# One more pair of tiles by seven products ahead of a scan, and fewer fillers inside it

## The chip, the cores and the metric

The kernel runs on one core of a Trainium2 chip. Its time is the device time of one execution in microseconds (us). The engines are TensorE (PE, with its weight loads listed as PEld), VectorE (DVE), ScalarE (ACT), GpSimd (POOL) and SyncE (SP, which here only issues transfers).

## What is computed

One layer of a bidirectional encoder over 1024 positions of width 1024, all in float32. The input is normalised and multiplied by one wide matrix; its 56 column tiles of 128 feed several mixers at once.

```python
h    = rmsnorm(x, attn_norm_w)
proj = h @ w_in                       # 1024 x 8192 columns
glu_in, q, v, z_f, z_b, og, g_a, g_b = split(proj)
a = dwconv31(glu(glu_in)); a = silu(layernorm(a)) @ pw_w
o = scan_forward(q, v, z_f) + scan_backward(q, v, z_b)   # 8 heads of 128, chunkwise
b = (rmsnorm_per_head(o) * silu(og)) @ o_w
x = x + (sigmoid(g_a) * a + sigmoid(g_b) * b) @ w_out
x = x + (silu(dwconv3(h2 @ w_gate)) * (h2 @ w_up)) @ w_down,  h2 = rmsnorm(x)
out = rmsnorm(x, final_norm_w)
```

The 8 tiles of glu_in are made first. The change concerns how the other 56 tiles (q, og, v, z_f, z_b, g_a, g_b, 8 each) are shared out.

## The kernel before

A product of a weight tile and the activations is three matrix multiplications of 128x512 (mm3, lines 148 to 150): each operand is split into a coarse part and a remainder, and high x high, high x low and low x high are added. The split itself (split, line 124) is a copy on ScalarE and a subtraction on VectorE.

Output tiles are made in two ways. A plain tile (std_job) takes 2 halves of the positions x 8 blocks x 3 = 48 multiplications. A pair (pair_job) makes two tiles together by a scheme of Strassen's kind: seven products of half the depth, 7 x 4 x 3 = 84 multiplications where two plain tiles need 96. It needs sums of weight blocks (add, lines 295 to 301: on VectorE with `first`, else by accumulating DMAs issued from GpSimd), seven split operands and combinations of the products (copy at line 428, evac at line 784).

The work is cut into pieces: a piece of these tiles is six multiplications, so that a pair has 14 pieces and a plain tile 8. TensorE's order is written out by hand: a Stream hands out pieces, and code that has other work for TensorE calls fill(n) between its steps. A fraction of a piece is kept as owed until the next call. The order on the other engines is made by a planner from costs and due times.

The stages around the change, in order:

- The convolution of 31 taps over 4 channel tiles runs on VectorE (conv_steps, taps at line 1023). The loop calls s_pairs.fill(CONV_FILL) after each of its 124 steps; the LayerNorm that follows has fills of its own (LN_FILL, 5, LN_LAST, twice), and then the stream of pairs is drained. NPAIRS pairs are made here; todo, the list of the 56 tiles, is taken in order.
- What is left of todo becomes plain tiles (rest_jobs), and after them 8 tiles of the convolution's pointwise product, 4 pieces each. They are the fillers of the scan (dense).
- The scan handles 8 heads x 2 halves = 16 items. For each item scan_levels has three steps and scan_states two; after each of these five, between(FILL) hands out FILL filler pieces, advances the preparation of the next item (scan_base) and the outputs of the head before (scan_outputs). Per item, TensorE forms block products at several levels: small ones (level, line 1179), then blocks of 32 and of 64 (blocks, line 1262), which read keys kG and queries qF that VectorE has just doubled (double_keys and double_queries, line 1128); then it transposes the keys (line 1302), ScalarE copies them (line 1304), and TensorE forms the states (line 1311). A head's outputs follow (line 1352). The value tile is transposed and copied once per item (line 1454).
- Before the loop, dense.fill takes 7 + 14 pieces; after it, TAIL takes 10 and the rest is drained.

```python
jobs = collections.deque(in_pair(n) for n in range(1, NPAIRS))
for _ in conv_steps():
    s_pairs.fill(CONV_FILL)
...
rest = todo[2 * NPAIRS :]
rest_jobs = [std_job(in_cols(c), ND, h_std, e) for c, e in rest[:-2]]
...
def between(fill):
    dense.fill(fill)
    if ahead is not None:
        ahead.step(BASE_STEPS)
    pending.fill(1)
```

Of the kernel before, what the change touches and what calls it, by code (L numbers as in the profile page):

```python
# [16 lines left out]
AX = mybir.AxisListType  # L17

P = 128
FILL = 1.77  # L20
TAIL = ((1, 2), (1, 1), (2, 4), (2, 3))
CONV_FILL = 1.67
NPAIRS = 19
LN_FILL = 6
LN_LAST = 12
GLU_FIRST = 4
# [21 lines left out]
def tile_hybrid_encoder(  # L48
# [201 lines left out]
    def std_job(src, nk, acts, evac, halves=(0, 1), step=2):  # L250


        def prep():
            raw = raw_w(src, nk)
            return split(w_page(nk), w_page(nk), raw, V)

        def run(w, halves=halves):
            for half in halves:
                acc = bank("mm")
                for k in range(nk):  # L260
                    mm3(acc, w, acts(k, half), k, k == 0, k == nk - 1)
                    if k % step == step - 1 or k == nk - 1:
                        yield
                evac(half, acc)

        return prep, run
# [299 lines left out]
    def in_cols(c0):  # L566
        return w_cols(w_in, 0, ND, c0)
# [246 lines left out]
    def in_pair(n):  # L814
        (c0, e0), (c1, e1) = todo[2 * n], todo[2 * n + 1]
        evs = (e0, e1)
        return pair_job(
            in_cols(c0),
            in_cols(c1),
            NK2,  # L820
            lambda i: ht[i],
            p1,
            p1,
            lambda e, *quadrant: evs[e](*quadrant),
            first=n == 0 or n >= 14,
            columns=2,
        )

# [121 lines left out]
    h_combos()  # L950
    s_glu.fill(GLU_LATE)
    pair0 = in_pair(0)
    w_pair0 = pair0[0]()
    s_glu.drain()
# [51 lines left out]


    jobs = collections.deque(in_pair(n) for n in range(1, NPAIRS))
    jobs.appendleft((lambda: w_pair0, pair0[1]))
    s_pairs = Stream(run_jobs(jobs, 4))  # L1010

    def conv_steps():
        for j in (3, 0, 1, 2):
            acc = p1.tile([P, S], F32, tag="ca", name=nm("acc"), bufs=2)
            g = gl[j]

            def tap(k):
                return vec("cdw", k * NCW + j)

            V.tensor_scalar(acc, g[:, 0:S], tap(0), vec("cb", j), op0=ALU.mult, op1=ALU.add)  # L1020
            yield
            for k in range(1, CK):
                V.scalar_tensor_tensor(  # L1023
                    acc, g[:, k : k + S], tap(k), acc, op0=ALU.mult, op1=ALU.add
                )
                yield
            for half in range(2):
                nc.sync.dma_start(d_cv[j][half], acc[:, half * H : (half + 1) * H])

    for _ in conv_steps():  # L1030
        s_pairs.fill(CONV_FILL)

# [39 lines left out]

    rest = todo[2 * NPAIRS :]
    rest_jobs = [std_job(in_cols(c), ND, h_std, e) for c, e in rest[:-2]]
# [220 lines left out]
    def scan_states(i, kG, v, Tt, Sf, Sb):  # L1295

        half = i % 2
        kTs = []
        for d in range(2):
            b = bank("mm" if d else "tr")  # L1300
            for c in range(4):
                T.transpose(b[:, c * P : (c + 1) * P], kG[:, d, c * P : (c + 1) * P], ident)
            kT = page(hp, "kT", 2)
            A.copy(kT, b)
            kTs.append(kT)
        yield
        for d in range(2):
            u = bank("mm" if d else "sc")
            for c in range(4):
                sl = slice(c * P, (c + 1) * P)  # L1310
                T.matmul(u[:, sl], kTs[d][:, sl], v[:, c, :], start=True, stop=True)
            u4 = c4(u)
            if d == 0:
                for c in range(4 if half == 0 else 3):
                    nx = Sf[half][:, c + 1, :] if c < 3 else Sf[1][:, 0, :]
                    if half == 0 and c == 0:
                        V.tensor_copy(nx, u4[:, 0, :])
                    else:
                        V.scalar_tensor_tensor(
                            nx,  # L1320
                            Sf[half][:, c, :],
                            Tt[:, half, 0, c : c + 1],
                            u4[:, c, :],
                            op0=ALU.mult,
                            op1=ALU.add,
                        )
            else:

                A.copy(Sb[half][:, 0:3, :], u4[:, 1:4, :])
                if half == 1:  # L1330
                    A.copy(Sb[0][:, 3, :], u4[:, 0, :])
        yield
# [96 lines left out]
    for h in range(NH):  # L1429
# [4 lines left out]
        for half in range(2):  # L1434
# [5 lines left out]
# [5 lines that stand above are left out]
# [3 lines left out]
            for n, _ in enumerate(scan_levels(base, S_t, Tt[:, half])):  # L1448
                if n == 1:
# [4 lines left out]
                    A.copy(v.rearrange("p c e -> p (c e)"), b)  # L1454
                between(FILL)
            qF, kG = base[:2]
            for _ in scan_states(i, kG, v, Tt, Sf, Sb):
                between(FILL)
            kept.append((S_t, v, qF))
# [481 lines left out]
    n = starts[-1] - per_seven - 12  # L1941
# [49 lines left out]
```

## Time and profile before

| What | us |
|---|---|
| median of 3 runs | 1755.64 (1755.04 to 1755.79) |
| the profiled execution | 1754.85 |
| its span, from the first to the last instruction | 1753.0 |
| TensorE busy | 1715.2 (98%) |
| VectorE busy | 1253.1 (71%) |
| ScalarE busy | 819.9 (47%) |
| mean granted TensorE clock | 0.996 of full speed |

A row of a table by stages gives the stretch in us from the span's start, its length, the busy time and number of instructions of PE, PEld, DVE, ACT and POOL, then the granted clock, the mean busy share of the 16 DMA engines and GB/s. In a group of instructions stand the line, the engine, the operation, output<-inputs, shapes and count, then busy time and the mean of one in ns, and after the bar the engine's idle time just before them with what ended it. A row of waits reads: who waited, for whom, us in total, times, the longest. The time of a multiplication in the list (some 390 ns) covers a pipeline; how far apart two of them start is the price of one.

### The profile page before, as it was taken

The page shows a single profiled execution, that of the slowest core. Times are in us where ns is not written, and L with a number is a line of the kernel's source. Part 1 is how long each engine was busy: PE and PEld are TensorE (multiplying, and loading weights), DVE is VectorE, ACT ScalarE, POOL GpSimd, SP SyncE. Part 2 cuts the span into 40 slices and gives each one's busy share as a digit, 9 for nine tenths or more (in the row PEclk, how much of TensorE's full clock was granted, in tenths as well). Part 3 has the DMA queues.
Part 4 walks back from the last instruction along what each step waited for, and adds up shares of the span by engine and source line. Part 5 has one row for each costly group of instructions (what it writes and reads, how often), then busy time and mean ns, then how long its engine had stood idle before and what let it go on. Part 6 is the DMA issues. An engine that isn't in the chain of part 4 may idle for free. (4 is left out here: it accounts for less than half of the span.)

```text
span 1753.0 us, 30378 instructions
## 1 busy us (share of the span) xinstructions
PE 1715.2 (98%) x11806; PEld 1409.3 (80%) x11806; DVE 1253.1 (71%) x1919; ACT 819.9 (47%) x1528; POOL 170.0 (10%) x184
## 2 busy tenths in 40 slices
PE   8999999999999999999999999999999999999997
PEld 6878888887888788788878887888878888878775
DVE  5599999746678888788556466676667777548864
ACT  7444433334466667776342245444334334443333
POOL 2201111100000000000000002111111111000110
PEclk9999999999999999999999999999999999999998
DMA  8768888855663343446579465586768776634742
GB/s 288 239 162 185 195 189 199 207 158 171 205 198 110 117 130 124 125 125 201 172 259 318 139 205 192 151 167 140 167 151 185 169 178 147 206 120 124 184 88 96
DMA packets 338470, 301.76 MB, mean 172 GB/s; under 512 B 24975, under 2 KB 252055, under 8 KB 338327
## 3 DMA queue, kind: packets, MB, share of 16 engines
q1 hardware_dynamic: 284310, 261.02, 47.5%
q0 software_dynamic: 44800, 37.76, 14.9%
q10 hardware_dynamic: 9216, 1.05, 0.4%
q8 instruction: 92, 1.51, 0.4%
q14 instruction: 52, 0.42, 0.1%
HBM read 197.27 MB, written 84.67 MB: 161 GB/s over the span
## 5 line engine op out<-in xcount | busy, mean ns | idle before, releaser
L148 PE MATMUL mm<-hx,wp 128*128 128x512 f32 x1068 | 428.2, 401 | 4.2 <-ACT tm L835 2.3
L150 PE MATMUL mm<-hx,wp 128*128 128x512 f32 x1068 | 418.0, 391 | 2.3 <-DVE wp L124 2.2
L149 PE MATMUL mm<-hx,wp 128*128 128x512 f32 x1068 | 417.1, 391 | 0.5 <-DVE hx L124 0.5
L124 ACT CAST wp<-wr 128x1024 fp32r<-128x1024 f32 (+2 forms) x147 | 147.3, 1003 | 261.8 <-PE mm L149 115.0
L148 PEld LDWEIGHTS mm<-hx,wp 128*128 128x128 f32 x1068 | 201.0, 188 | 48.3 <-ACT tm L835 2.8
L150 PEld LDWEIGHTS mm<-hx,wp 128*128 128x128 f32 x1068 | 200.8, 188 | 47.6 <-DVE wp L124 4.7
L149 PEld LDWEIGHTS mm<-hx,wp 128*128 128x128 f32 x1068 | 201.2, 188 | 40.5 <-DVE hx L124 1.2
L124 DVE TENSOR_TENSOR wp<-wr,wp 128x1024 fp32r<-128x1024 f32 (+2 forms) x145 | 169.6, 1170 | 75.0 <-ACT wp L124 68.4
L1023 DVE SCALAR_TENSOR_TENSOR acc<-gl,v_b,acc 128x1024 f32<-128x1024 f32 x120 | 149.2, 1282 | 0.4
L428 ACT COPY su<-mm 128x512 f32<-128x512 f32 x82 | 47.6, 581 | 65.2 <-PE mm L150 65.2
L1128 DVE TENSOR_TENSOR qF<-qF,tb 128x512 f32<-128x512 f32 x96 | 65.2, 687 | 11.7 <-ACT A L1160 11.7
L148 PE MATMUL tr<-hx,wp 128*128 128x512 f32 x180 | 70.5, 392 | 0.0
L124 ACT CAST wq<-sw 128x1024 fp32r<-128x1024 f32 x41 | 43.1, 1051 | 58.3 <-PE mm L149 43.0
L150 PE MATMUL tr<-hx,wp 128*128 128x512 f32 x180 | 70.1, 389 | 0.0
L149 PE MATMUL tr<-hx,wp 128*128 128x512 f32 x180 | 70.0, 389 | 0.0
L1618 DVE SCALAR_TENSOR_TENSOR tm<-gp,v_a,tm 128x512 f32<-128x512 f32 x88 | 66.0, 750 | 4.2 <-ACT tm L1616 2.0
L1128 DVE TENSOR_TENSOR kG<-kG,tb 128x512 f32<-128x512 f32 x96 | 65.7, 687 | 3.8 <-PE sc L1262 3.8
L148 PE MATMUL mm<-hy,wp 128*128 128x512 f32 x164 | 64.5, 393 | 0.0
L149 PE MATMUL mm<-hy,wp 128*128 128x512 f32 x164 | 64.2, 392 | 0.0
L148 PE MATMUL sc<-hy,wq 128*128 128x512 f32 x164 | 64.2, 392 | 0.0
L150 PE MATMUL sc<-hy,wq 128*128 128x512 f32 x164 | 64.2, 391 | 0.0
L149 PE MATMUL sc<-hy,wq 128*128 128x512 f32 x164 | 63.8, 389 | 0.0
(372 smaller groups left out, 3571.9 us busy)
## 6 DMA issues: line engine op xcount, KB each, us to landing
wr<-in_w_in_dram SPq DMA_DIRECT2D x48, 512.0 KB, 4.7
wr<-in_ffn_w_up_dram SPq DMA_DIRECT2D x22, 512.0 KB, 4.5
sw<-in_w_in_dram SPq DMA_DIRECT2D x38, 256.0 KB
d_g<-ft SPq DMA_DIRECT2D x38, 256.0 KB, 3.3
sw<-in_ffn_w_up_dram SPq DMA_DIRECT2D x38, 256.0 KB, 3.4
sw<-in_ffn_w_up_dram POOLq DMA_DIRECT2D x19, 512.0 KB, 8.4
wr<-sw POOLq DMA_DIRECT2D x32, 256.0 KB, 3.4
wr<-wr POOLq DMA_DIRECT2D x32, 256.0 KB, 3.9
```

The lines of the kernel that those rows point to most:

```text
L124: parts = A.copy(hi, src), eng.tensor_tensor(lo, src, hi.bitcast(F32), op=ALU.subtract)
L148: T.matmul(acc, whi[:, k, :], ahi, start=first, stop=False, skip_group_check=again)
L149: T.matmul(acc, whi[:, k, :], alo, start=False, stop=False, skip_group_check=again)
L150: T.matmul(acc, wlo[:, k, :], ahi, start=False, stop=last, skip_group_check=again)
L428: A.copy(t, acc)
L1023: V.scalar_tensor_tensor(acc, g[:, k : k + S], tap(k), acc, op0=ALU.mult, op1=ALU.add)
L1128: V.tensor_tensor(o, a, b, op=op)
L1618: V.scalar_tensor_tensor(c, g[:, o + k : o + k + H], vec("fdw", k * NF + j), c, op0=ALU.mult, op1=ALU.add,)
```

## The change

Twenty pairs are made ahead of the scan instead of 19; the tiles that move are z_f and z_b of the last head, which were the first two fillers. So 16 plain tiles instead of 18 stay as fillers, 160 pieces in all instead of 176, and each step of the scan hands out 1.56 pieces instead of 1.77. The convolution's steps hand out 1.78 pieces instead of 1.67. The pairs whose weight sums are made on VectorE are 0 and 15 to 19 instead of 0 and 14 to 18; pair 14's sums are now made by DMA.

```diff
-FILL = 1.77
+FILL = 1.56
 TAIL = ((1, 2), (1, 1), (2, 4), (2, 3))
-CONV_FILL = 1.67
-NPAIRS = 19
+CONV_FILL = 1.78
+NPAIRS = 20
...
             lambda e, *quadrant: evs[e](*quadrant),
-            first=n == 0 or n >= 14,
+            first=n == 0 or n >= 15,
             columns=2,
```

## The prediction

> **What bounds the kernel now.** First the head of the page, then busy time by stage.
>
> ```profile
> span 1753.0 us, 30378 instructions
> PE 1715.2 (98%) x11806; PEld 1409.3 (80%) x11806; DVE 1253.1 (71%) x1919; ACT 819.9 (47%) x1528; POOL 170.0 (10%) x184
> ```
>
> TensorE (PE) is the only engine that is busy nearly throughout. The change moves work from one stage into another, so I read the two stages separately: the stretch in which the pairs run beside the convolution and its LayerNorm (100 to 500 us), and the scan's loop over 16 items (519 to 856 us, from the first to the last copy of v at L1454).
>
> ```profile
> core 0: us, PE busy (x) PEld busy (x) DVE busy (x) ACT busy (x) POOL busy (x), PEclk, DMA share, GB/s
> 100.00:340.00 240.00, 239.37 (x1050) 197.41 (x1050) 230.74 (x245) 93.95 (x131) 39.84 (x40) 1.00 0.80 186
> 340.00:500.00 160.00, 159.15 (x702) 129.96 (x700) 93.42 (x129) 72.26 (x112) 6.08 (x8) 1.00 0.61 192
> ...
> 519.10:855.60 336.50, 329.94 (x5415) 276.90 (x5415) 267.32 (x587) 227.36 (x521) 12.85 (x14) 1.00 0.43 130
> ```
>
> In the pair stretch PE idles 1.5 us of 400; in the scan 6.6 us of 336.5. So both stages follow PE, but the scan has a second engine close behind: VectorE (DVE) is busy 267 of 336.5 us there. What PE waits for in the scan, and what a full-rate stretch of pairs looks like:
>
> ```profile
> PE sc L1262 <- DVE qF L1128: 4.2, 7, 1.0
> PE sc L1311 <- ACT kT L1304: 2.3, 2, 1.4
> ```
>
> ```profile
> 200.00:250.00 50.00, 50.00 (x222) 41.42 (x221) 48.75 (x48) 20.75 (x30) 8.36 (x8) 1.00 0.77 176
> 250.00:300.00 50.00, 50.00 (x223) 41.38 (x222) 49.89 (x48) 17.18 (x25) 9.13 (x8) 1.00 0.87 200
> ```
>
> The waits are 6.5 us together, and the first names the link that matters: the block products of L1262 need queries that VectorE has just doubled (L1128). The second fence gives PE's price: 50.00 us by 223 products is 0.224 us for one of 128x512 at the full granted clock (1.00).
>
> **The change part by part: TensorE.** A pair by seven products is 7 x 4 x 3 = 84 multiplications. The two filler tiles that leave the scan are 2 tiles x 2 halves x 8 x 3 = 96. The pair goes into the stretch that PE fills: 84 x 0.224 = +18.8 us. The price of a filler in the scan is read between two products eight steps apart:
>
> ```profile
> 633.63 0.40 PE L148 MATMUL mm<-hx,wp 128*128 128x512 f32 x1
> ...
> 635.46 0.39 PE L150 MATMUL mm<-hx,wp 128*128 128x512 f32 x1
> ```
>
> 1.83 us by 8 is 0.229 us, so 96 x 0.229 = -21.9 us, if PE sets the pace of all that remains. Sum: -3.1 us. The Trainium skill (TensorE: Matmul & The Clock Gate, section Back-to-back issue gap) gives a sustained spacing of about 131 ns for 512 columns; by it the same sum would be an estimated -1.6 us. The trace does not agree with that figure, 224 ns being the steady spacing of these products, and I use the trace.
>
> **The pair's other work**, nearly all under cover. For each pair VectorE runs three splits of 1024 columns, one of 512 and three combinations of 512 (all L124 and L784), where two plain tiles take two splits of 1024.
>
> ```profile
> L124 DVE TENSOR_TENSOR wp<-wr,wp 128x1024 fp32r<-128x1024 f32 x15 | 18.3, 1222 | 5.5 <-ACT wp L124 5.2
> L297 DVE TENSOR_TENSOR sw<-sw,sw 128x1024 f32<-128x1024 f32 x5 | 6.1, 1226 | 13.2 <-DMA sw<-in_w_in_dram 7.4 <-DMA w<-in_w_in_dram 3.5 <-DMA d_v<-ev 2.3
> L784 DVE TENSOR_TENSOR ev<-sc,su 128x512 f32<-128x512 f32 x8 | 5.5, 688 | 3.4 <-PE sc L150 3.4
> ```
>
> That is 3 x 1.22 + 4 x 0.69 = 6.4 us per pair. In 340 to 500 us VectorE idles 67 us, so it is hidden; without that cover it would cost the 6.4 us. The moved bound (n >= 15) leaves six pairs with their sums on VectorE, as now (L297 x5 here, and pair 0); pair 14 makes its three sums by accumulating DMAs from POOL's queue:
>
> ```profile
> wr<-sw POOLq DMA_DIRECT2D x32, 256.0 KB, 3.4
> wr<-wr POOLq DMA_DIRECT2D x32, 256.0 KB, 3.9
> ...
> sw<-in_w_in_dram POOLq DMA_DIRECT2D x13, 512.0 KB, 8.5
> ```
>
> 8.5 + 3.4 + 3.9 = 15.8 us one after another, against 18.8 us of the pair before it, in a stretch where POOL is busy 6 us of 160 and nothing else waits on its queue. Pairs 1 to 13 do the same now, with a fuller VectorE, and PE lost 0.6 us in 240. I price it at 0; if it came late it would cost up to its first transfer, 8.5 us. SP issues 1.75 MB for a pair instead of 1 MB for two tiles; DMA is at 0.61 there, so 0.
>
> **The convolution's taps** move 1.78 instead of 1.67 pieces apart in program order, but only PE's order is written by hand. In the order of the built program VectorE's queue still carries 11 taps or so beside each of pairs 1 to 9 and the last one beside pair 11, as before the change. So this constant does next to nothing there: 0, within 1 us either way. The LayerNorm that follows is spread by its own, unchanged fills.
>
> **The scan.** between(FILL) runs 80 times (five steps, 16 items). 80 x 1.77 gives 141 pieces of six products; 1.56 gives 124. Around the loop 35 pieces become 36. Steps with one piece only go from 19 to 36 of 80. What goes is 17 pieces in the loop, 23.4 us of PE, just where VectorE is nearest. Each item has a place where PE needs VectorE twice (L1262, blocks of 32 and of 64). The stretch that ends at the first L1262 of the first item of a head, counted from the second L1262 of the item before, is VectorE's long one:
>
> ```profile
> 585.70:603.60 17.90, 16.54 (x294) 13.32 (x294) 16.59 (x36) 12.71 (x24) 0.00 (x0) 1.00 0.54 166
> 632.20:648.40 16.20, 16.18 (x282) 13.37 (x286) 16.17 (x35) 11.52 (x22) 0.00 (x0) 1.00 0.60 180
> 677.10:693.20 16.10, 16.10 (x291) 13.30 (x294) 15.15 (x35) 11.75 (x22) 0.00 (x0) 1.00 0.54 169
> ...
> 768.10:784.30 16.20, 16.16 (x298) 13.42 (x302) 15.63 (x37) 10.67 (x21) 0.00 (x0) 1.00 0.48 148
> ```
>
> The other item of a head leaves VectorE more room; from its second L1262 to the next item's:
>
> ```profile
> 654.70:677.10 22.40, 22.40 (x367) 18.87 (x366) 15.69 (x34) 17.60 (x47) 1.83 (x2) 1.00 0.36 110
> ```
>
> In the long stretch of 16.2 us VectorE is busy 15.2 to 16.2; the first row already pays 1.4 us of PE idle. In the new order this stretch has 36 filler products instead of 42 in most heads, so PE would need 16.2 - 1.4 = 14.8 us, while VectorE's instructions there fall only from about 34 to about 32, at 0.46 us each (16.17 by 35): 14.3 to 15.3 us of work, to which its own waits on other engines come (17.90 - 16.59 = 1.3 us in the first row). It would end between 0.5 us before PE and 1.8 us after it. Bounds over eight heads: 0, or 8 x 1.4 = 11 us if nothing removed there is gained. I take 0.4 us a head, below the middle, because three of the four rows show hardly a wait now: 3.2 us. The second place is the step between the two L1262:
>
> ```profile
> 632.22 0.69 PE L1262 MATMUL sc<-qF,kG 128*64 128x64 f32 x16 [0.59 <-DVE qF L1128]
> ```
>
> Here one piece lay between and PE waited 0.59 us (the longest such wait above is 1.0). Such steps go from three to six: 3 x 0.6 = 1.8 us. Added waits: 3.2 + 1.8 = 5.0 us.
>
> **Sum.** -3.1 + 5.0 = +1.9 us. The profiled execution took 1754.85 us (span 1753.0 and 1.85 around it), the median of the runs is 1755.64; the sum made on the profile, 1756.75, is 1757.5 us in terms of the median. For all chances, "no change" is within 0.2%, 3.5 us, about what a measurement of this kernel can tell from none: 1752.1 to 1759.2 us.
>
> **The rivals.**
> 1. The scan's waits do not grow, or shrink. The planner has ordered VectorE's queue anew, and a better place for the doubling would free part of the 6.5 us that PE waits now. For it: in the third and fourth row above PE loses nothing. Against it: the busy shares of 94 to 100%. Time: 1755.6 - 3.1 = 1752.5 with waits as now, 1749.3 with half of them gone. Chance 0.26, of which 0.20 lie below 1752.1.
> 2. VectorE becomes the pace of the scan, and the filler taken out is replaced by idle time. For it: the row of 585.7 to 603.6 us. It decides from 6.6 us of added waits on (3.1 + 3.5), that is 0.8 us a head. With all eight long stretches unshortened and 1.8 us at the short steps the sum is -3.1 + 11 + 1.8 = +9.7, 1765.3; halfway from that point it is about 1762. Against it: VectorE idles 69 us in the loop, and in the other item of a head 6.7 us of 22.4, where lateness is made good. Chance 0.34.
> 3. Pair 14's accumulating DMAs come late. The Trainium skill (SBUF — State Buffer, section SBUF: two separate sides) says that VectorE can keep GpSimd from writing the descriptors of DMAs that it issues. As a mechanism here: VectorE's sums or LayerNorm passes hold the three issues, and the pair's first transfer stands open, 1757.5 + 6 to 8.5, some 1765. The trace speaks against it: from 250 to 300 us VectorE was busy 49.89 us of 50, POOL issued eight, and PE did not stop. Chance 0.02.
>
> That the change does not do what it says holds for the taps alone, and changes no number.
>
> **How the numbers follow.** My forecast, waits grown by 3 to 6.6 us, has 0.38. Faster by over 0.2%: 0.20, from rival 1. Within: 0.38 and the remaining 0.06 of rival 1, 0.44. Slower: 0.34 and 0.02, 0.36. The range leaves out about a tenth at each end: from 1751.5, inside rival 1, to 1764, most of rival 2. The forecast's own range is 1755.5 to 1759.2.
>
> **What would show it.** Right: the stage up to the scan 18 to 20 us longer, the products there still 0.224 us apart; a loop of 16 items, 22.4 us each now, at 21.2 to 21.4 us instead of the 20.9 that PE alone would allow; PE's waits in the scan 10 to 13 us instead of 6.5, nearly all at L1262 on qF; VectorE busy around 83% in the loop, from 79%. Wrong: PE's waits there at 6 us or less (rival 1), above 13 us (rival 2), or a gap in the products of the 340 to 520 us stretch in front of pair 14 (rival 3).
>
> ```profile
> L1454 ACT COPY v<-tr x16: 572/581/588, 519.1 to 855.6; 128x512 f32<-128x512 f32 x16
> ```
>
> This row gives the 22.4 us: 336.5 us by 15 intervals; 17 pieces by 16 items are 1.06 pieces, 1.46 us less PE work in each.

## The result and the profile after

| Kernel | Median, us | Runs | Ratio to before, 95% interval |
|---|---|---|---|
| before, on the same chip | 1755.79 (1754.83 to 1758.82) | 7 | |
| changed | 1761.32 (1759.23 to 1765.12) | 7 | 1.0033 [1.0023, 1.0043] |

The change makes the kernel slower by 0.33%, 5.5 us. That lies inside the range of 1751.5 to 1764, but the likeliest case was "within 0.2%", and this is past it. The profiled execution of the changed kernel took 1762.16 us, 7.3 more than that of before. Head of its page:

```profile
span 1760.4 us, 30368 instructions
PE 1713.8 (97%) x11794; PEld 1407.7 (80%) x11794; DVE 1256.3 (71%) x1924; ACT 819.6 (47%) x1530; POOL 172.3 (10%) x187
```

TensorE has 12 multiplications less, as counted, and is busy 1.4 us less; the span grew by 7.4. So all of the loss is time in which TensorE waits. By stages, columns as before; the last row is a short piece inside the first stage:

```profile
100.00:340.00 240.00, 236.98 (x1035) 194.69 (x1034) 229.52 (x243) 91.86 (x129) 39.68 (x39) 0.99 0.79 184
340.00:520.30 180.30, 180.18 (x795) 147.60 (x794) 99.84 (x136) 78.45 (x122) 8.46 (x11) 1.00 0.64 193
539.40:861.10 321.70, 309.43 (x5319) 259.27 (x5318) 264.29 (x585) 222.90 (x515) 12.84 (x14) 1.00 0.42 130
304.90:308.30 3.40, 3.40 (x10) 2.62 (x9) 3.40 (x5) 0.00 (x0) 0.00 (x0) 0.50 0.60 199
```

TensorE's idle time in the loop went from 6.6 to 12.3 us (321.70 - 309.43). The loop became 14.8 us shorter instead of the 21.9 that the 96 multiplications were to bring. Beside the convolution TensorE now idles 3.0 us of 240 where it idled 0.6. From the first pair's second product to the first copy of v the trace gives 400.7 us before and 423.2 after: +22.5 for a pair reckoned at 18.8. What follows the loop took 899.3 instead of 897.4, and the first pair started 2.2 us earlier. Together: -2.2 + 22.5 - 14.8 + 1.9 = +7.4, the difference of the spans.

Two of these terms hold the same loss. In the short row above, TensorE's clock was granted at half for 3.4 us, which costs some 1.7 us. Before has such a stretch too, but ahead of its first pair, where it delays that pair:

```profile
98.80:102.20 3.40, 3.40 (x10) 2.67 (x9) 2.90 (x5) 1.24 (x2) 0.40 (x3) 0.51 0.42 123
```

So 1.7 us of the 22.5 only changed places, out of what stands ahead of the pairs.

TensorE's longest waits, whole execution:

```profile
PE sc L1262 <- DVE qF L1128: 8.8, 11, 1.8
...
PE mm L148 <- DVE ev L784: 3.0, 3, 1.8
PE mm L148 <- ACT hx L124: 2.7, 1, 2.7
PE ob L1352 <- DVE Sb L1404: 2.6, 2, 2.1
```

The first row stood at 4.2 us. The second is in the pair stretch and the third behind the loop; the fourth, in the loop, has no row among the loop's waits of before.

**In the scan.** The first three rows are stretches from a second L1262 to the first L1262 of a head's first item (the long stretches of the prediction), the last two lead to the other item of a head:

```profile
602.70:618.80 16.10, 15.33 (x293) 12.34 (x294) 14.80 (x32) 11.94 (x23) 0.00 (x0) 1.00 0.59 185
691.50:706.90 15.40, 14.97 (x292) 12.32 (x293) 15.23 (x33) 10.67 (x21) 0.00 (x0) 1.00 0.60 178
734.80:752.10 17.30, 15.08 (x290) 12.08 (x290) 15.50 (x34) 11.41 (x23) 0.00 (x0) 1.00 0.48 151
625.00:643.20 18.20, 16.97 (x311) 14.36 (x311) 13.11 (x32) 15.47 (x44) 1.83 (x2) 1.00 0.38 112
713.10:730.60 17.50, 16.89 (x307) 14.30 (x306) 11.06 (x27) 13.94 (x39) 1.83 (x2) 1.00 0.37 112
```

In before, one long stretch that the prediction doesn't show lost time too:

```profile
721.70:740.10 18.40, 16.47 (x298) 13.22 (x297) 16.25 (x37) 13.05 (x24) 0.00 (x0) 1.00 0.54 162
```

Over the whole loop the seven long stretches lose 3.7 us (0.8, 0.4, 2.2 in the rows above, 0.3 in one more, nothing in three), where those of before lost 3.3 (1.4 and 1.9, nothing in five). That is hardly more. The steps between the two L1262 lose 5.4 instead of 1.7 us, 2.1 of them in one wait of L1352. The stretches to the other item lose 3.2 instead of 1.6, and in those that lose VectorE idles 5.1 to 6.5 us. A full VectorE can't be what delays it there. This is the beginning of another theory.

**In the pair stretch.** VectorE's queue around the longest of the three waits, then TensorE there:

```profile
295.38 5.24 DVE L1023 SCALAR_TENSOR_TENSOR acc<-gl,v_b,acc 128x1024 f32<-128x1024 f32 x4
303.15 0.69 DVE L1035 TENSOR_TENSOR tm<-cx 128x512 f32<-128x512 f32 x1 [2.53 <-DMA cx<-d_cv]
303.76 0.68 DVE L784 TENSOR_TENSOR ev<-su,mm 128x512 f32<-128x512 f32 x1
```

```profile
302.29 0.39 PE L150 MATMUL sc<-hx,wq 128*128 128x512 f32 x1
304.50 0.50 PE L148 MATMUL mm<-hx,wp 128*128 128x512 f32 x1 [1.82 <-DVE ev L784]
304.83 0.59 PE L149 MATMUL mm<-hx,wp 128*128 128x512 f32 x1
305.22 0.63 PE L150 MATMUL mm<-hx,wp 128*128 128x512 f32 x1
```

A sum of the LayerNorm (L1035) waits 2.53 us for data on their way back from DRAM. Behind it in VectorE's queue stands the evacuation that frees TensorE's bank (L784), and TensorE stops.

### The profile page after: what moved, and what is told of

Same layout as the page of the kernel before. It is cut to its first block, busy times and chain, and to the rows that moved or that the text cites. A ratio compares the mean times of both kernels' runs of the same rounds, so it can differ in the third digit from the quotient of the medians.

```text
span 1760.4 us, 30368 instructions
## 1 busy us (share of the span) xinstructions
PE 1713.8 (97%) x11794; PEld 1407.7 (80%) x11794; DVE 1256.3 (71%) x1924; ACT 819.6 (47%) x1530; POOL 172.3 (10%) x187
## 4 chain that ended last, share of the span: by engine, by line
PE 44%; issue 2%; DMA 2%; DVE 1%; ACT 1%; POOL 0%; POOLq 0%; SPq 0%; ACTq 0%; DVEq 0%
PE mm L148 10%; PE mm L150 10%; PE mm L149 10%; PE sc L148 3%; PE sc L150 3%; PE sc L149 3%; PE tr L148 1%; PE tr L150 1%; PE tr L149 1%; DMA wr<-in_ffn_w_down_dram 1%; DMA tm<-d_bm 0%; DVE hx L124 0%; DMA ft<-d_t 0%; DVE gx L124 0%; ACT hx L124 0%
## 5 line engine op out<-in xcount | busy, mean ns | idle before, releaser
L148 PE MATMUL mm<-hx,wp 128*128 128x512 f32 x1044 | 418.7, 401 | 8.3 <-DVE ev L784 3.0
L150 PE MATMUL mm<-hx,wp 128*128 128x512 f32 x1044 | 408.6, 391 | 3.6 <-DVE wp L124 3.4
L149 PE MATMUL mm<-hx,wp 128*128 128x512 f32 x1044 | 407.8, 391 | 0.0
L148 PEld LDWEIGHTS mm<-hx,wp 128*128 128x128 f32 x1044 | 196.5, 188 | 52.2 <-DVE ev L784 4.8
L150 PEld LDWEIGHTS mm<-hx,wp 128*128 128x128 f32 x1044 | 196.3, 188 | 47.9 <-DVE wp L124 5.9
L149 PEld LDWEIGHTS mm<-hx,wp 128*128 128x128 f32 x1044 | 196.6, 188 | 38.4 <-issue 0.7
L1128 DVE TENSOR_TENSOR qF<-qF,tb 128x512 f32<-128x512 f32 x96 | 64.9, 685 | 14.0 <-ACT A L1160 14.0
L148 PE MATMUL tr<-hx,wp 128*128 128x512 f32 x184 | 72.5, 394 | 0.0
L150 PE MATMUL tr<-hx,wp 128*128 128x512 f32 x184 | 71.6, 389 | 0.0
L149 PE MATMUL tr<-hx,wp 128*128 128x512 f32 x184 | 71.6, 389 | 0.0
L1128 DVE TENSOR_TENSOR kG<-kG,tb 128x512 f32<-128x512 f32 x96 | 65.4, 684 | 3.0 <-PE sc L1262 2.8
L148 PE MATMUL sc<-hy,wq 128*128 128x512 f32 x168 | 65.8, 392 | 0.0
L150 PE MATMUL sc<-hy,wq 128*128 128x512 f32 x168 | 65.7, 391 | 0.0
L149 PE MATMUL sc<-hy,wq 128*128 128x512 f32 x168 | 65.3, 389 | 0.0
```

The source lines that it names most:

```text
L148: T.matmul(acc, whi[:, k, :], ahi, start=first, stop=False, skip_group_check=again)
L149: T.matmul(acc, whi[:, k, :], alo, start=False, stop=False, skip_group_check=again)
L150: T.matmul(acc, wlo[:, k, :], ahi, start=False, stop=last, skip_group_check=again)
L1128: V.tensor_tensor(o, a, b, op=op)
```

## The experiments

Three theories of the scan's waits were tried.

- Theory 1, the prediction's: VectorE has too much to do there; less work on it shortens the waits.
- Theory 2: a chain of short steps between VectorE and ScalarE sets the time, through what ScalarE's queue holds. A doubling (L1128) waits for a copy by ScalarE (L1160), and ScalarE is held by the four DMAs per item that it issues at L1292.
- Theory 3: it matters at which of an item's five steps the filler pieces lie.

The rows behind theory 2. First how L1292's issues stand in the changed kernel's trace (count, then min, median and max in ns), then who waits in the loop, in before (first two) and in the changed kernel (last two), and one place in the timeline:

```profile
L1292 ACTq DMA_DIRECT2D S<-D x64: 592/608/1813, 543.5 to 867.5; - x64
```

```profile
DVE qF L1128 <- ACT A L1160: 11.7, 7, 2.7
...
ACT A L1160 <- DMA S<-D: 5.1, 2, 2.8
```

```profile
DVE qF L1128 <- ACT A L1160: 14.0, 7, 2.8
...
ACT A L1160 <- DMA S<-D: 9.4, 3, 3.9
```

```profile
648.71 2.67 ACTq L1292 DMA_DIRECT2D S<-D  x4
...
651.47 0.62 ACT L1160 COPY A<-qF 128x512 f32<-128x512 f32 x1 [2.79 <-DMA S<-D]
...
652.12 0.69 DVE L1128 TENSOR_TENSOR qF<-qF,tb 128x512 f32<-128x512 f32 x1 [0.99 <-ACT A L1160]
```

Each issue holds ScalarE for 0.61 us, 64 of them for 39 us, which the busy time doesn't count. At 651.47 ScalarE's copy has waited 2.79 us, the length of the four issues ahead of it, and VectorE's doubling waits for that copy.

All runs together. "Pairs" goes from the first pair's second product to the first copy of v, "loop" from the first to the last copy of v, both from the profiled execution; "idle" is the loop less TensorE's busy time in it.

| Run | Median, us | Ratio to before | Pairs | Loop | Idle |
|---|---|---|---|---|---|
| before | 1755.79 | | 400.7 | 336.5 | 6.6 |
| changed | 1761.32 | 1.0033 [1.0023, 1.0043] | 423.2 | 321.7 | 12.3 |
| e1, before with FILL 1.56 | 1766.57 | 1.0056 [1.0044, 1.0068] | 401.9 | 320.0 | 10.9 |
| e2, changed, CONV_FILL 1.67 | 1762.45 | 1.0032 [1.0020, 1.0044] | 420.2 | 320.9 | 11.4 |
| e3, changed, key scale on ScalarE | 1764.87 | 1.0041 [1.0027, 1.0054] | 422.8 | 321.8 | 12.3 |
| e4, before, key scale on ScalarE | 1755.75 | 0.9994 [0.9985, 1.0002] | 403.5 | 334.5 | 5.1 |
| e5, changed, L1292 on SyncE | 1759.47 | 1.0011 [1.0002, 1.0020] | 422.9 | 314.4 | 6.0 |
| e6, changed, pieces shared anew | 1768.26 | 1.0062 [1.0046, 1.0078] | 424.7 | 321.9 | 12.7 |
| e7, changed, LayerNorm sums pinned | 1765.82 | 1.0047 [1.0035, 1.0059] | 419.6 | 320.5 | 11.6 |
| e8, before, pieces shared anew | 1749.97 | 0.9962 [0.9949, 0.9975] | 402.2 | 329.3 | 1.8 |
| e9, before, L1292 on SyncE | 1754.64 | 0.9980 [0.9970, 0.9990] | 402.5 | 332.8 | 3.3 |
| e10, changed, L1292 on GpSimd | 1755.87 | 0.9997 [0.9984, 1.0009] | 422.7 | 312.4 | 6.1 |
| e11, e8 with L1292 on SyncE | 1751.05 | 0.9966 [0.9954, 0.9979] | 403.1 | 328.1 | 0.9 |
| e12, changed, both | 1756.21 | 0.9996 [0.9985, 1.0008] | 426.1 | 310.8 | 3.8 |

Before was run beside each: 1756.39 us for e1 to e4, 1756.93 for e5 to e8, 1757.03 for e9 to e12. Runs of one kernel spread by 0.1 to 0.5%, so a ratio resolves some 2 us, and single profiles less. One thing by which profiles differ can be read in them: each holds one to three stretches of 3.41 us at half the clock, in places that change from kernel to kernel. In the pair stretch they stand in the changed kernel, e6 and e12 alone. What follows the loop took 897.4 to 899.3 us where it holds none (before, changed, e2, e8), 898.7 to 902.7 with one (e3, e4, e6, e9, e10, e11) and 900.5 to 904.0 with two (e5, e7, e12); e1 has the moved pieces there.

**e1: the filler alone.** The pieces leave the loop and follow it. Nothing else changes in the program, but the planner puts VectorE's instructions in another order (see the reservation below).

```diff
-FILL = 1.77
+FILL = 1.56
```

> Before, with FILL = 1.56 alone: 19 pairs as before, 17 filler pieces (102 products, 23.4 us) leave the scan's loop and run after it, so TensorE's work is the same. Theory 1 (in the scan VectorE becomes late at L1262 when filler is taken out): the loop from the first to the last copy of v falls from 336.5 us to 319 to 323, not to 313, TensorE's waits there are 11 to 15 us instead of 6.5, and the whole is 5 to 9 us slower than before. Rival (the loss of the change lies in the pair stretch, where VectorE waits for stores and loads of the convolution and TensorE idles): the loop falls to 313 to 315 us and the whole is within 2 us of before.

```profile
519.40:839.40 320.00, 309.15 (x5319) 259.51 (x5318) 261.19 (x579) 223.70 (x516) 12.83 (x14) 1.00 0.40 124
PE sc L1262 <- DVE qF L1128: 7.7, 9, 1.5
```

Moving 17 pieces to behind the loop (96 multiplications less between its first and last copy of v) makes the kernel 0.56% slower, 9.8 us, with the same work in it. The loop is as short, and its idle time nearly as long, as with 20 pairs. So of the 5.7 us that the changed kernel idles more in the loop, 4.3 come with the thinner filler alone, without the pair.

**e2: the taps' constant.**

```diff
-CONV_FILL = 1.78
+CONV_FILL = 1.67
```

> The changed kernel with CONV_FILL put back to 1.67. Theory 1: the scan is untouched, its loop 320 to 323 us, the whole within 2 us of the changed kernel (1759 to 1763). Rival (the wider spacing of the taps brings VectorE's waits for the convolution's stores and loads, and TensorE's idle time behind them, near 243 and 303 us of the changed trace): those gaps shrink to the 0.9 us of before and the whole falls by 2 to 4 us.

The wait behind L1035 is shorter in this profile:

```profile
PE mm L148 <- DVE ev L784: 0.8, 1, 0.8
```

It is 3.0 to 5.1 us in all six profiles with 20 pairs, 1.78 and this sum unpinned, and 0.5 to 2.8 in those with 1.67. The pair stretch is 3.0 us shorter than in the changed kernel, and 2.5 to 2.7 us shorter than in e3, e5 and e10, which like e2 have no stretch at half the clock there. The median doesn't follow: 1.0032 against 1.0033, where 3 us would be 0.0017 and the intervals are 0.0010 to 0.0012 either way. The profiled execution (1759.44) is the fastest of the five that the median of 1762.45 rests on. So the constant does move a wait, which I had excluded; whether the whole time gains from undoing it stays open.

**e3 and e4: less work for VectorE.** The scale of the keys goes into an activation of ScalarE; k = c - c sigmoid(z) is the same key.

```diff
-            A.activation(kG[:, d, :], z, AF.Sigmoid, scale=-1.0)
             A.activation(z, z, AF.Sigmoid)
+            A.activation(kG[:, d, :], z, AF.Identity, scale=kneg[...], bias=kscale[...])
...
-            V.tensor_scalar(kG[:, d, :], kG[:, d, :], ks[:, d : d + 1], None, op0=ALU.mult)
```

> The changed kernel with less VectorE work in the scan: the key's scale (L1208, two VectorE instructions of 0.48 us per item) is folded into ScalarE's making of the key, k = c - c*sigmoid(z), which costs ScalarE some 0.2 us more for each. 15.5 us leave VectorE in the loop. Theory 1: TensorE's waits at L1262 fall from 8.8 us to 2 to 5, the loop from 321.7 to 314 to 318 us, the whole by 3 to 8 us (1753 to 1758). Rival (the loss is in the pair stretch): loop and whole change by less than 1.5 us.

> The same fold in the kernel before. Its scan waits 6.5 us. Theory 1: a gain of 1 to 4 us (1752 to 1755), less than with 20 pairs, so that 20 pairs against 19 is then between -3 and +2 us. Rival: no gain in either, and 20 pairs stay 5 us slower.

The loop of e3 (L1266 is the former L1262, L1166 the former L1160):

```profile
542.10:863.90 321.80, 309.55 (x5319) 260.31 (x5318) 252.46 (x560) 222.83 (x511) 14.32 (x14) 0.99 0.42 130
PE sc L1266 <- DVE qF L1128: 10.9, 8, 3.2
DVE qF L1128 <- ACT A L1166: 22.7, 15, 2.8
```

VectorE works 11.8 us less than in the changed kernel (252.46 against 264.29), and TensorE waits as long as ever. VectorE spends the time waiting for ScalarE's copies: 22.7 us instead of 14.0. With 19 pairs (e4) nothing is gained that the interval shows. Theory 1 falls.

**e5, e9 and e10: L1292 out of ScalarE's queue.**

```diff
-            nc.scalar.dma_start(S_t[g : g + 32, :, g : g + 32], D_t[g : g + 32])
+            nc.sync.dma_start(S_t[g : g + 32, :, g : g + 32], D_t[g : g + 32])
```

In e10 it reads nc.gpsimd.dma_start.

> The changed kernel with the four small transfers per item that build the score tile (L1292) issued by SyncE instead of ScalarE. The key-scale run showed that less VectorE work does not shorten the waits at L1262, and that VectorE itself waits there for ScalarE's copies (L1160). Theory 2 (the waits come from the ping-pong of VectorE and ScalarE, whose queue is held some 2.6 us an item by these four issues): TensorE's waits at L1262 fall from 8.8 us to 3 to 6, the loop from 321 us to 315 to 319, the whole by 3 to 6 us. Theory 3 (what counts is only how much filler lies in the two steps ahead of L1262): loop and whole within 1.5 us of the changed kernel, or slower where SyncE's queue now holds loads back.

> The kernel of before with 19 pairs and its filler as it is; only the transfers of line 1292 are issued by SyncE instead of ScalarE. If the chain through ScalarE's queue sets the waits before line 1262 (theory 2), the waits of ScalarE for S<-D (5.1 us in before) and of VectorE's qF for A (11.7) go, and the loop (336.5) comes to 332 to 334, the time to about 1754 to 1755. If the gain of e5 came from something that only 20 pairs have, such as the order that the planner gave VectorE there, the time stays within 0.1% of before.

> The changed kernel, with the transfers of line 1292 issued by GpSimd instead of ScalarE. VectorE's order is nearly that of e5. If it is ScalarE's queue that has to be cleared of them, the loop is as in e5, 314 to 317 us, and the time about 1759, whichever engine takes them. If SyncE is what helped (its queue is faster than GpSimd's), L1311 or L1262 wait for S<-D and the loop stays at 320 or more.

The loops, in the order e5, e9, e10:

```profile
541.20:855.60 314.40, 308.38 (x5319) 259.68 (x5319) 263.13 (x585) 223.12 (x514) 12.85 (x14) 1.00 0.43 133
PE sc L1262 <- DVE qF L1128: 5.0, 6, 1.0
DVE qF L1128 <- ACT A L1160: 0.7, 2, 0.5
```

```profile
518.80:851.60 332.80, 329.50 (x5415) 277.23 (x5415) 266.27 (x588) 227.78 (x521) 12.86 (x14) 1.00 0.43 132
PE sc L1262 <- DVE qF L1128: 3.2, 6, 1.0
DVE qF L1128 <- ACT A L1160: 0.4, 1, 0.4
```

```profile
540.10:852.50 312.40, 306.29 (x5320) 257.66 (x5318) 263.47 (x587) 222.86 (x515) 46.28 (x74) 1.00 0.43 134
PE sc L1262 <- DVE qF L1128: 6.0, 8, 1.2
```

VectorE and ScalarE do the same work as in the kernels that these were made from, yet with 20 pairs the loop is 7.3 (e5) and 9.3 us (e10) shorter. VectorE's wait for ScalarE's copies is down from 14.0 to 0.7 us, and no wait of ScalarE for S<-D is left in the three. It works with 19 pairs too (e9, 0.9980), and with either other queue. GpSimd pays for the issues openly, 46.28 us busy instead of 12.84, and has the room. e10 beat its expectation of 1759 by 3 us. The changed kernel comes to 0.9997 of before this way.

The Trainium skill (Perfetto Trace Analysis, section DMA Optimizations) says that spreading DMAs over the engines that can issue them may help where the issuing engine looks busy with issues rather than transfers. The three runs agree, and add that the queue needn't be full for it: ScalarE's issues took 39 of 322 us.

One reservation, and it holds for every experiment but e2 and e7: the planner, which sees the cost of issuing, also put VectorE's instructions in another order. Of its instructions in the loops of both traces, 50% are followed by the same one in e9 as in before, 43% in e5 as in the changed kernel, 91% in e10 as in e5. For e1 it is 20% as in before and 66% as in the changed kernel, for e8 25% as in before. That the waits on S<-D and on the copies went is shown; that the new orders had no part in the times, those of e1 and e8 above all, is not.

**e6 and e8: the same number of pieces, shared otherwise.** More pieces at the two steps ahead of the first and the second L1262, fewer at the others; e8 with 141 pieces in 16 items, e6 with 124.

```diff
+STEPS = (2.0, 2.0, 1.55, 1.65, 1.65)    # e8;  e6: (2.0, 2.0, 1.0, 1.4, 1.4)
...
-                between(FILL)
+                between(STEPS[n])
...
-            for _ in scan_states(i, kG, v, Tt, Sf, Sb):
-                between(FILL)
+            for n, _ in enumerate(scan_states(i, kG, v, Tt, Sf, Sb)):
+                between(STEPS[3 + n])
```

> The changed kernel with the same 124 pieces in the loop, but always two in each of the two steps ahead of the products of L1262, and one or two in the other three (2, 2, 1, 1.4, 1.4 on the mean instead of 1.56 each). Theory 3: waits at L1262 fall from 8.8 to 2 to 5 us, the loop to 314 to 318 us, the whole by 3 to 7 us, to the time of before or 2 us under it. Theory 2: TensorE only meets the same lateness of the chain elsewhere, the waits move to other lines, loop within 2 us of 321.

> The kernel before with the same 141 pieces in the loop, two in each of the steps ahead of L1262 and 1.55 to 1.65 in the others. Theory 3: before's waits at L1262 (4.2 us) fall to 1 to 3, the whole by 1 to 3 us. Theory 2: no change within 1.5 us.

First e6, then e8 (lines one higher):

```profile
PE sc L1312 <- ACT kT L1305: 8.7, 7, 1.8
...
PE sc L1263 <- DVE qF L1129: 0.4, 1, 0.4
DVE qF L1129 <- ACT A L1161: 24.4, 14, 3.6
```

```profile
519.80:849.10 329.30, 327.51 (x5410) 275.39 (x5409) 264.98 (x585) 226.80 (x520) 12.85 (x14) 1.00 0.43 133
PE sc L1263 <- DVE qF L1129: 0.7, 2, 0.5
DVE qF L1129 <- ACT A L1161: 14.5, 9, 2.9
```

With 141 pieces the waits all but vanish, and e8 is 0.38% faster than before, the best of all and more than the 1 to 3 us expected. VectorE still waits 14.5 us for ScalarE there: the chain is as long, but TensorE has something to do meanwhile. With 124 pieces the wait at L1262 vanishes too, and comes back at L1311, behind a step of one piece and one of 1.4 (they had 1.56 each). That share was a poor one, and at 1.0062 worse than none. Together they fit theory 3 as long as there is enough to share.

**e7: the LayerNorm's sums in program order.** L1035 and the sums that follow it (L1037) are kept from moving ahead of the evacuations.

```diff
-        V.tensor_tensor(o, ts[0], ts[1], op=ALU.add)
+        pin(V.tensor_tensor(o, ts[0], ts[1], op=ALU.add))
...
-            V.tensor_tensor(o, o, t, op=ALU.add)
+            pin(V.tensor_tensor(o, o, t, op=ALU.add))
```

> The changed kernel with the LayerNorm's first sums (L1035, L1037) kept in program order on VectorE, so that L1035 no longer stands among the last taps, waiting for a load (2.5 us at 300 us of the changed profile), with TensorE's operands behind it. If the pair stretch loses time to that wait: the stretch from the first pair's second product to the first copy of v falls from 420 to 423 us to 418 to 420, the whole by 1 to 3 us. If the gaps there are only the difference of single executions: no change within 1 us.

L1035 no longer waits for its data, and the pair stretch is 3.6 us shorter, as in e2. The time is not better but, if anything, worse (1.0047). What the pinned order costs elsewhere was not found. In its profile the part behind the loop is 904.0 us instead of 899.3, but 3.4 of these 4.7 us are its two stretches at half the clock, of which the changed kernel's profile has none there.

**e11 and e12: both remedies.** e11 is e8 with L1292 on SyncE; e12 is the changed kernel with L1292 on SyncE and STEPS = (1.7, 1.7, 1.4, 1.5, 1.5).

> The kernel of before with both: its 141 filler pieces shared 2, 2, 1.55, 1.65, 1.65 over the five steps (as in e8) and the transfers of line 1292 issued by SyncE. In e8 TensorE's waits in the loop are down to 1.8 us, so if the waits are all that is to be had, the second part adds at most 1.5 us: 1748.5 to 1750. If the transfers on SyncE cost elsewhere (they stand among its weight loads), it is 1751 or more.

> The changed kernel with the transfers of line 1292 issued by SyncE and its 124 pieces shared 1.7, 1.7, 1.4, 1.5, 1.5 over the five steps. With the chain shortened, fewer fillers are needed at each step: if chain and cover together are the whole cause of the lost gain, TensorE's waits in the loop fall from 5 us (e5) to 3 or less, the loop to 311 to 313, and the time to 1755 to 1758, about that of before. If 124 pieces don't cover five steps however they are shared, waits move to L1311 as in e6 and the loop stays at 315 to 318, the time at 1759 or more.

The loop of e12:

```profile
543.10:853.90 310.80, 307.05 (x5318) 258.92 (x5317) 263.45 (x586) 222.72 (x515) 12.86 (x14) 1.00 0.43 135
PE sc L1263 <- DVE qF L1129: 3.3, 4, 1.6
```

e12's loop and time came as expected, with idle time of 3.8 us where waits of 3 or less were expected, and a time that can't be told from before. e11 adds nothing to e8 (0.9966 against 0.9962), as there was 1.8 us of idle time left to win. Its 1751.05 us lie at the mark for transfers that cost something elsewhere on SyncE; the difference to e8 is within what ratios resolve, so that stays open. Side by side, with the chain short and the pieces well shared in both, 20 pairs still lose 0.30% to 19. By the profiles: the loop is 17.3 us shorter, the pair stretch 22.9 longer. The idle time in the loop is 2.8 us of that. In the pair stretch TensorE's wait on L784 is 5.1 us in e12 against 1.1 in e11, and behind the longest of these waits e12 has a stretch at half the clock, some 1.7 us, that e11 has not.

## Why the prediction was right and wrong

- **The pair, +18.8.** The 84 multiplications are there, 0.227 us apart where nothing stalls (19.1 us). They are so in before as well: the 0.224 of the prediction divides 50 us by 223 products, of which the first two only reach into the stretch. The stretch grew by 22.5 us. With CONV_FILL at 1.67 (e2) it is 420.2 us, 17.9 more than the mean of the six kernels with 19 pairs (402.3).
- **The taps, "0, within 1 us".** This step failed in the traces. I had counted the taps in VectorE's queue and not looked at what else stands in it: L1035, waiting for DRAM ahead of an L784. TensorE's wait on L784 rose from 0.5 to 3.0 us, its idle time in the stretch by 1.6, and 1.7 us are the half clock after the longest wait: 3.3 of the 3.4 us beyond the pair's own 19.1. That size rests on profiles; the medians of e2 and e7 don't confirm it.
- **The fillers, -21.9.** The count of 96 is right (96 x 0.229 is 22.0, not 21.9). TensorE's busy time in the loop fell by 20.5 us, 1.4 less than reckoned.
- **The waits in the scan, +5.0.** The idle time rose by 5.7 us, and of the marks set the waits (12.3 us idle, 10 to 13 expected, though 8.8 at L1262 instead of nearly all) and VectorE (82%) came out (83% expected); an item takes 21.45 us (321.7 by 15), just above the 21.2 to 21.4. That the sum came near is luck, for its terms were wrong. The long stretches were to lose 3.2 us more and lose 0.4 more; the prediction had left out a row of before that already lost 1.9. The steps between the two L1262 were to add 1.8 and add 3.8. The stretches to the other item, which was to have room, add 1.6. The reason was wrong too: the waits don't follow VectorE's amount of work (e3) but the chain between VectorE and ScalarE (e5, e9, e10) and the filler that covers it (e1, e6, e8), as far as the planner's new orders had no part in that.
- **Pair 14's DMAs, 0.** No product waited for them: 180.18 us busy of 180.30 from 340 us on. Rival 3 did not come. Nor does TensorE wait for a sum or a split anywhere in the pair stretch.
- **Rival 2** was to give a slower kernel through more than 6.6 us of added waits in the scan. The kernel is slower, the added waits are 5.7. What took it past the 0.2% is the sum: against the -3.1 + 5.0 of the prediction, 3.7 us more in the pair stretch, 2.1 less won in the loop, 1.9 more behind it, and 2.2 less at the start, 5.5 us in the profiles and 3.6 in the medians. Of the 3.7 and of the 2.2, 1.7 us are the stretch at half the clock that changed places. The 1.9, and what is left of the 2.2, are within what varies from one kernel's profile to the next.

So the amount in the scan was near for a wrong reason. By the profiles the forecast was missed by about as much in the pair stretch (2.0 us without the half clock) as in the loop (2.1).

## What to carry to other kernels

Filler work between the steps of a latency chain is not only work: it is the cover of the chain, and what is taken out there pays less than its own time (here 14.8 of 21.9 us). Before removing it, look at where each piece lies, and at what the chain waits for; the same pieces shared otherwise gained 0.38%, and four DMA issues an item, moved to another queue, 0.20%, each with the planner's new order along with it. An engine that idles 5 us of 18 can still be the one that comes late, so read who it waits for, not how busy it is.

## What the hardware showed beside that

- Issuing a DMA holds the issuing engine's queue for 0.61 us on ScalarE, and for 0.59 to 0.60 us on SyncE (medians of 64). In the profile it shows as the next instruction's wait for that DMA's output, though that instruction needs nothing from it.
- After the gap of 2.21 us at 302.3 us (1.82 us of it idle) nine products came slower, the third to the ninth of them 0.43 us apart, and then 0.23 again; the row of 304.9 to 308.3 us shows a granted clock of 0.50. After a gap of 1.39 us in the same stretch they came 0.34 and then 0.24 apart. The Trainium skill (TensorE: Matmul & The Clock Gate, section Part 1: The HAM clock gate) gives 426.7 ns for 512 columns at half the clock, which agrees, and has the clock halved after an idle window of about 3.4 us; here a gap of 2.21 us was enough. But the length alone doesn't decide: the wait of 2.7 us behind the loop of the same trace was not followed by half a clock (from 900 to 906 us it was 1.00).
- The stretches at half the clock last 3.41 us in all fourteen traces, between the first and the last products. A pair of profiles is compared fairly only when it is known where they lie.
